# Rotary queries of a latent-attention layer: formed with channels on partitions, two heads at a time, with turned tables

## The chip, the core and the metric

One NeuronCore of a Trainium2 chip runs the whole kernel. The metric is the device time of one execution in microseconds; the shown time is the median of three runs. Everything is in 32-bit floats. A product that needs more precision than one pass of TensorE gives is made of three: each operand is split into a high half (rounded to the matmul's format, fp32r) and a low half (the rest), and high x low, low x high and high x high are added up in PSUM.

## The reference, cut to what matters

One layer: a token mixer of three branches and a gated MLP. The change lies in branch B, multi-head latent attention with 8 heads over 512 positions; each head has 128 plain channels and 64 rotary ones.

```python
def _apply_rope(x, cos, sin):
    x1, x2 = jnp.split(xf, 2, axis=-1)
    return jnp.concatenate([x1 * cos - x2 * sin, x2 * cos + x1 * sin], axis=-1)

def _mla(cq, ckv, kr, cos, sin, g_q, w_uq, g_kv, w_ukv):
    q = jnp.einsum('bsr,rhd->bshd', _rms_norm(cq, g_q), w_uq)
    kv = jnp.einsum('bsr,rhd->bshd', _rms_norm(ckv, g_kv), w_ukv)
    q_nope, q_rope = q[..., :QK_NOPE], q[..., QK_NOPE:]
    k_nope, v = kv[..., :QK_NOPE], kv[..., QK_NOPE:]
    q_rope = _apply_rope(q_rope, cos[:, :, None, :], sin[:, :, None, :])
    k_rope = _apply_rope(kr, cos, sin)
    scale = (QK_NOPE + QK_ROPE) ** -0.5
...
        s = (jnp.einsum('bqhd,bkhd->bhqk', q_nope[:, q0:q1], k_nope[:, :q1])
             + jnp.einsum('bqhd,bkd->bhqk', q_rope[:, q0:q1], k_rope[:, :q1]))
        s = s.astype(jnp.float32) * scale
...
        p = jax.nn.softmax(s, axis=-1).astype(v.dtype)
        outs.append(jnp.einsum('bhqk,bkhd->bqhd', p, v[:, :q1]))
```

## The kernel before, in words

All activations lie as tiles of 128 partitions x 512. The modulated input is hT (channels on partitions, 8 tiles, each with a high and a low half). The latent projections come out with positions on partitions, are normalised (cn), turned by TensorE transposes (ptc) and split into cT0, cT1 (the query latent, 256 channels) and cT2 (the key and value latent), each with h and l. The shared rotary key is turned in the same way: krT holds its high half twice, on partitions 0 to 63 and 64 to 127, krL its low half on 0 to 63 and zeros below.

Rotary queries of before: `rotary_queries` (L646) loads and splits the weight wqr as a whole, and for each of the four blocks of 128 positions forms pq (128 positions x 8 heads x 64 channels) by six matmuls of 512 columns, with the positions on partitions. VectorE multiplies pq by the scaled cosines and sines, cosQ and sinQ (made on ScalarE at L239 and L240), GpSimd subtracts and adds the halves into qro, and ScalarE and VectorE split the result into a high and a low half that lie side by side in a staging tile qst, 128 columns a head. `rotary_transposes` (L684) then turns one head: four transposes into ptq, one copy out into qrT (high half on partitions 0 to 63, low half on 64 to 127). Heads 0 to 3 are turned ahead of the head loop, heads 4 to 7 inside it, after the scores of the head four before.

`scores(h)` multiplies qrT by krL and by krT, so that high and low halves of the query meet the key in one pass each, and adds the plain part, q by k. In the head loop stand, for each head, the weights of the next head, its scores, the attention of the head before (`attend`), the projection of the next head (`project`: q and k from cT), one gate (24 matmuls, `mm_chunk`, L110) and the transposes of the softmax.

What sets the order: the code is written in program order, and a scheduler places each engine's instructions; an engine then takes its own in that order and waits at the first one whose inputs are not there. So an instruction that waits holds up all that stand behind it on its engine. PSUM has eight tiles (pool `pp`), taken in turn. Weights come by SyncE's DMA into three raw tiles; ScalarE casts the high half (L92), VectorE subtracts for the low half (L93), and two pairs of split tiles are used in turn.

Of the kernel before, what the change touches and what calls it, by code (L numbers as in the profile page):

```python
# [8 lines left out]
F32 = mybir.dt.float32  # L9
F32R = mybir.dt.float32r  # L10
# [40 lines left out]
def trunk(ctx: ExitStack, tc: tile.TileContext, A, out):  # L51
# [21 lines left out]
    def pt_t(name, dt=F32):  # L73
        return sb.tile([P, 512], dt, name=name, tag="pt", bufs=8)
# [4 lines left out]
    def f(ap):  # L79
        return ap.bitcast(F32)  # L80

    def load(src, n, name):
        raw = wp.tile([P, D], F32, name=name, tag="raw", bufs=3)
        with tc.issue_after(last_load[0]):
            nc.sync.dma_start(out=raw[:, :n], in_=src)
        return raw

    def wsplit(src, n, name):
        raw = load(src, n, name)
        hi = wp.tile([P, D], F32R, name=name + "h", tag="whi")  # L90
        lo = wp.tile([P, D], F32R, name=name + "l", tag="wlo")
        nc.scalar.copy(out=hi[:, :n], in_=raw[:, :n])  # L92
        ins = nc.vector.tensor_tensor(  # L93
            out=lo[:, :n], in0=raw[:, :n], in1=f(hi[:, :n]), op=ALU.subtract
        )
        last_lo[:] = [ins.ins]
        return hi, lo
# [7 lines left out]
    def mm3(o, wh, wl, xh, xl, start, stop):  # L105
        nc.tensor.matmul(o, wh, xl, start=start, stop=False)
        nc.tensor.matmul(o, wl, xh, start=False, stop=False)
        return nc.tensor.matmul(o, wh, xh, start=False, stop=stop)
# [80 lines left out]
    with tc.issue_after(x_load.ins):  # L189
# [13 lines left out]
    cosT, sinT, cosQ, sinQ = (  # L203
        const.tile([P, TT, 32], F32, name=name) for name in ("cosT", "sinT", "cosQ", "sinQ")
    )

    def angles():
        posf = const.tile([P, TT], F32, name="posf")
# [18 lines left out]
    def sines():  # L227
        nc.vector.tensor_scalar(
            out=ang, in0=ang, scalar1=3.1415925, scalar2=-3.1415925, op0=ALU.min, op1=ALU.max
        )  # L230
        nc.scalar.activation(sinT, ang, AF.Sin)
        nc.vector.scalar_tensor_tensor(
            out=kq, in0=ang, scalar=-1.0, in1=ang, op0=ALU.mult, op1=ALU.max
        )
        nc.vector.tensor_scalar(
            out=kq, in0=kq, scalar1=-1.0, scalar2=1.5707963267948966, op0=ALU.mult, op1=ALU.add
        )
        nc.scalar.activation(cosT, kq, AF.Sin)
        nc.scalar.activation(cosQ, cosT, AF.Copy, scale=SCALE)  # L239
        nc.scalar.activation(sinQ, sinT, AF.Copy, scale=SCALE)  # L240

    first_raw = {}
    first_acc = {}
# [327 lines left out]
    with after_split():  # L571
# [4 lines left out]
    ss = const.tile([P, TT, 2], F32, name="ss")  # L576
    rr = const.tile([P, TT, 2], F32, name="rr")
    cqn = []
    tA, tB, ro, krl = (
        act_t(name, F32)[:, : TT * 64].rearrange("p (t c) -> p t c", c=64)  # L580
        for name in ("tA", "tB", "ro", "krl")
    )
    kr = act_t("kr", F32).rearrange("p (t c) -> p t c", c=128)
# [52 lines left out]
    nc.scalar.copy(out=krF, in_=pt[:, 0:P])  # L636
    pt = ps("ptk")
    for t in range(TT):
        nc.tensor.transpose(pt[0:64, t * P : (t + 1) * P], krl[:, t, :], ident)
    nc.vector.tensor_copy(out=krL[0:64, :], in_=pt[0:64, :])  # L640
    nc.gpsimd.memset(f(krL[64:128, :]), 0.0)


    qrs = []

    def rotary_queries():  # L646
        wh, wl = wsplit(A["wqr"], D, "wqr")
        for t in range(TT):
            pq = ps("pq")
            ts_ = slice(t * P, (t + 1) * P)  # L650
            for k in range(2):
                c = slice(k * 512, (k + 1) * 512)
                mm3(pq, cT_hi[k][:, ts_], cT_lo[k][:, ts_], wh[:, c], wl[:, c], k == 0, k == 1)
            tA = pt_t("qtA")
            tB = pt_t("qtB")
            src = pq.rearrange("p (a b) -> p a b", b=32)
            for dst, tab in ((tA, cosQ), (tB, sinQ)):
                nc.vector.tensor_tensor(
                    out=dst.rearrange("p (a b) -> p a b", b=32), in0=src,
                    in1=tab[:, t : t + 1, :].broadcast_to([P, 16, 32]), op=ALU.mult,  # L660
                )
            vA = tA.rearrange("p (h a b) -> p h a b", a=2, b=32)
            vB = tB.rearrange("p (h a b) -> p h a b", a=2, b=32)
            ro = pt_t("qro")
            vo = ro.rearrange("p (h a b) -> p h a b", a=2, b=32)
            nc.gpsimd.tensor_tensor(
                out=vo[:, :, 0, :], in0=vA[:, :, 0, :], in1=vB[:, :, 1, :], op=ALU.subtract
            )
            nc.gpsimd.tensor_tensor(
                out=vo[:, :, 1, :], in0=vA[:, :, 1, :], in1=vB[:, :, 0, :], op=ALU.add  # L670
            )
            st = [act_t(f"qst{t}{i}", F32) for i in range(2)]
            for i in range(2):
                dst = st[i].rearrange("p (h a b) -> p h a b", a=2, b=64)
                s4 = ro[:, i * 256 : (i + 1) * 256].rearrange("p (h b) -> p h b", b=64)
                nc.scalar.copy(out=dst[:, :, 0, :].bitcast(F32R), in_=s4)
                nc.vector.tensor_tensor(
                    out=dst[:, :, 1, :], in0=s4, in1=dst[:, :, 0, :], op=ALU.subtract
                )
            qrs.append(st)  # L680

    qrT = []

    def rotary_transposes(h):  # L684
        pt = ps("ptq")
        for t in range(TT):
            nc.tensor.transpose(
                pt[:, t * P : (t + 1) * P], qrs[t][h // 4][:, (h % 4) * P : (h % 4 + 1) * P], ident
            )
        q = act_t(f"qrT{h}")  # L690
        if h % 2:
            nc.vector.tensor_copy(out=q, in_=pt)
        else:
            nc.scalar.copy(out=q, in_=pt)
        qrT.append(q)


    V = {}
# [878 lines left out]
```

## Time and profile before

| what | value |
| --- | --- |
| median of 3 runs | 963.16 us (961.87 to 963.17) |
| the profiled execution's own time | 962.52 us |
| its span, first to last instruction | 960.8 us |
| mean granted TensorE clock | 0.998 |
| HBM traffic | 116.83 MB read, 2.10 MB written, 124 GB/s over the span |

In the views, PE is TensorE's matmuls, PEld its weight loads, DVE VectorE, ACT ScalarE, POOL GpSimd, SP SyncE. A timeline row has the start and the duration in us, the engine, the source line, the operation, what is written and read, the form, and in brackets how long the engine had been idle and what ended that. Neighbouring matmuls overlap, so what one takes of PE's time is read from start to start. A row of a stretch has the stretch, its length, then for each engine the busy time and the count, PE's granted clock, the share of the DMA engines and GB/s.

The busy tenths of the span in 40 slices of 24 us; the rotary queries lie in the third and fourth slices, the head loop in the fourth to the ninth:

```profile
PE   7999999999999999999999999999999999999996
DVE  7967556456686566477333489576565564732368
ACT  4575656543333322233332245554444444322121
POOL 4752110122350023202212712021111121766653
```

### The profile page before, as it was taken

What the parts mean: (1) busy time and instruction counts of PE and PEld (TensorE: products, weight loads), DVE (VectorE), ACT (ScalarE), POOL (GpSimd) and SP (SyncE); (2) the same over time, 40 slices, a digit from 0 to 9 for tenths busy, and PEclk for the clock granted to TensorE, in tenths of its full rate; (3) what the DMA queues carried; (4) which work ended last, traced back from release to release, by engine and by line L of the source; (5) the groups of instructions that cost most, each with busy time, mean ns of one, the idle gap of its engine ahead of it and who ended that gap; (6) DMA issues with size and microseconds to landing.
All of it is one profiled execution on the core that took longest, in us unless ns stands there. A gap on an engine that the chain in (4) does not pass through costs nothing.

```text
span 960.8 us, 12195 instructions
## 1 busy us (share of the span) xinstructions
PE 947.2 (99%) x4583; PEld 800.2 (83%) x4583; DVE 585.0 (61%) x849; ACT 386.3 (40%) x637; POOL 284.6 (30%) x257
## 2 busy tenths in 40 slices
PE   7999999999999999999999999999999999999996
PEld 6988888888888888888888889988888888888885
DVE  7967556456686566477333489576565564732368
ACT  4575656543333322233332245554444444322121
POOL 4752110122350023202212712021111121766653
PEclk9999999999999999999999999999999999999999
DMA  9822112044435643564343550143434433342222
GB/s 330 309 63 89 50 61 82 24 124 162 146 106 197 202 128 88 164 199 151 111 130 111 148 181 23 47 129 116 126 110 130 133 113 107 106 132 92 89 87 88
DMA packets 46139, 119.72 MB, mean 125 GB/s; under 512 B 5504, under 2 KB 8960, under 8 KB 46080
## 3 DMA queue, kind: packets, MB, share of 16 engines
q1 hardware_dynamic: 45648, 118.39, 38.4%
q8 instruction: 36, 0.59, 0.2%
q10 hardware_dynamic: 432, 0.55, 0.2%
q14 instruction: 23, 0.19, 0.1%
HBM read 116.83 MB, written 2.10 MB: 124 GB/s over the span
## 4 chain that ended last, share of the span: by engine, by line
PE 93%; DVE 2%; POOL 1%; ACT 1%; DMA 1%; issue 1%; POOLq 0%; SPq 0%; ACTq 0%
PE pzu L114 7%; PE pzu L113 7%; PE pzu L116 7%; PE pg L113 4%; PE pg L114 4%; PE pg L116 4%; PE py L113 4%; PE py L114 4%; PE py L116 4%; PE pyd L1150 3%; PE pyd L1148 3%; PE pyd L1151 3%; PE lat L531 2%; PE pu L113 2%; PE pu L114 2%; PE pa L113 2%
## 5 line engine op out<-in xcount | busy, mean ns | idle before, releaser
L93 DVE TENSOR_TENSOR wupl<-wup,wuph 128x1024 fp32r<-128x1024 f32 x38 | 48.1, 1267 | 71.9 <-PE pzu L116 42.7
L1117 POOL TENSOR_TENSOR d<-d,gtfb 128x512 f32<-128x512 f32 x44 | 74.4, 1713 | 35.9 <-DMA d<-in_wdn 34.0
L1420 POOL TENSOR_TENSOR zc<-zc 128x512 f32<-128x512 f32 x22 | 29.6, 1348 | 174.6 <-ACT zc L1419 132.5
L1122 DVE TENSOR_TENSOR dl<-d,dh 128x1024 fp32r<-128x1024 f32 x18 | 28.6, 1588 | 56.2 <-PE pyd L1148 52.0
L92 ACT CAST wuph<-wup 128x1024 fp32r<-128x1024 f32 x38 | 39.9, 1051 | 47.1 <-PE pzu L114 47.1
L422 POOL TENSOR_TENSOR mg<-mg,th 128x512 f32<-128x512 f32 x16 | 31.4, 1959 | 85.8 <-DVE th L419 85.8
L92 ACT CAST wbh<-wb 128x1024 fp32r<-128x1024 f32 x24 | 25.3, 1054 | 74.0 <-PE py L114 55.3
L93 DVE TENSOR_TENSOR wgl<-wg,wgh 128x1024 fp32r<-128x1024 f32 x22 | 30.0, 1365 | 37.4 <-ACT wgh L92 18.4
L871 DVE SCALAR_TENSOR_TENSOR ada<-adar,cact,ada 128x512 f32<-128x512 f32 x56 | 49.0, 906 | 1.5 <-DMA adar<-in_ada 1.5
L786 POOL TENSOR_SCALAR pe<-pe,mx 128x128 f32<-128x128 f32 (+3 forms) x32 | 17.1, 537 | 96.0 <-DVE mx L785 59.9
L1121 ACT CAST dh<-d 128x1024 fp32r<-128x1024 f32 x18 | 19.0, 1053 | 61.6 <-PE pyd L1151 32.3
L1402 ACT ACTIVATE zc<-pzu,cols 128x512 f32<-128x512 f32 x44 | 34.2, 780 | 22.3 <-PE pzu L116 17.8
L93 DVE TENSOR_TENSOR wbl<-wb,wbh 128x1024 fp32r<-128x1024 f32 x24 | 30.9, 1288 | 14.6 <-ACT wbh L92 6.5
L1405 DVE SCALAR_TENSOR_TENSOR zc<-pzu,cols,zc 128x511 f32<-128x511 f32 x44 | 32.6, 742 | 4.0 <-ACT zc L1402 4.0
L1409 DVE SCALAR_TENSOR_TENSOR zc<-pzu,cols,zc 128x510 f32<-128x510 f32 x44 | 32.6, 744 | 0.8
L419 DVE SCALAR_TENSOR_TENSOR th<-th,py 128x512 f32<-128x512 f32 x16 | 11.0, 686 | 35.7 <-PE py L116 35.7
L92 ACT CAST wgh<-wg 128x1024 fp32r<-128x1024 f32 x22 | 23.2, 1054 | 23.1 <-PE pg L114 18.5
L1419 ACT ACTIVATE zc<-zc 128x512 f32<-128x512 f32 x22 | 13.9, 631 | 41.4 <-DVE zc L1409 41.3
L924 POOL TENSOR_TENSOR asum<-apad 128x527 f32<-128x527 f32 x8 | 12.7, 1587 | 54.2 <-ACT apad L919 27.6
L300 DVE SCALAR_TENSOR_TENSOR acc<-ada,cact,acc 128x256 f32<-128x256 f32 (+1 forms) x29 | 26.6, 917 | 1.1
L1096 POOL TENSOR_TENSOR oraw<-oraw,gttb 128x512 f32<-128x512 f32 x6 | 10.5, 1775 | 47.9 <-DMA oraw<-in_wo 43.8
L1117 POOL TENSOR_TENSOR o<-o,gttb 128x512 f32<-128x512 f32 x10 | 16.6, 1681 | 13.2 <-DMA o<-in_wo 10.4
(1547 smaller groups left out, 3109.8 us busy)
## 6 DMA issues: line engine op xcount, KB each, us to landing
wup<-in_wup SPq DMA_DIRECT2D x44, 512.0 KB, 3.6
adar<-in_ada SPq DMA_DIRECT2D x64, 256.0 KB, 4.0
wb<-in_wb SPq DMA_DIRECT2D x24, 512.0 KB, 3.6
wg<-in_wg SPq DMA_DIRECT2D x22, 512.0 KB, 3.6
d<-in_wdn SPq DMA_DIRECT2D x22, 512.0 KB, 3.6
ada<-in_ada1p SPq DMA_DIRECT2D x24, 256.0 KB, 4.7
wa<-in_wa SPq DMA_DIRECT2D x8, 512.0 KB, 3.5
wsg<-in_wsg SPq DMA_DIRECT2D x8, 512.0 KB, 3.7
```

Of the source, the lines that this page charges most:

```text
L92: nc.scalar.copy(out=hi[:, :n], in_=raw[:, :n])
L93: ins = nc.vector.tensor_tensor(out=lo[:, :n], in0=raw[:, :n], in1=f(hi[:, :n]), op=ALU.subtract)
L113: nc.tensor.matmul(o, wh[:, c], xl[k], start=k == 0, stop=False)
L114: nc.tensor.matmul(o, wh[:, c], xh[k], start=False, stop=False)
L116: nc.tensor.matmul(o, wl[:, c], xh[k], start=False, stop=k == KT - 1)
L422: nc.gpsimd.tensor_tensor(out=merged[m], in0=merged[m], in1=th, op=ALU.add)
L871: nc.vector.scalar_tensor_tensor(out=acc[n], in0=src, scalar=cact[:, k : k + 1], in1=acc[n], op0=ALU.mult, op1=ALU.add,)
L1117: nc.gpsimd.tensor_tensor(out=halves[n], in0=halves[n], in1=gt[n], op=ALU.mult)
L1402: nc.scalar.activation(t, pz, AF.Identity, bias=cols[:, cc + 3 : cc + 4], scale=cols[:, cc + 2 : cc + 3])
L1405: nc.vector.scalar_tensor_tensor(out=t[:, 1:512], in0=pz[:, 0:511], scalar=cols[:, cc + 1 : cc + 2], in1=t[:, 1:512], op0=ALU.mult, op1=AL ...
L1409: nc.vector.scalar_tensor_tensor(out=t[:, 2:512], in0=pz[:, 0:510], scalar=cols[:, cc : cc + 1], in1=t[:, 2:512], op0=ALU.mult, op1=ALU.add,)
L1420: nc.gpsimd.tensor_tensor(out=val, in0=val, in1=gate, op=ALU.mult)
```

## The change

The rotary queries are formed with the channels on partitions: `rotary(p)` makes pq as 128 channels of two heads (2p and 2p + 1) x 512 positions, with wqr as the left operand and cT as the right one, again by six matmuls of 512 columns. The rotation now runs over partitions: qtA is pq times a turned table cosR; qtB takes, for each group of 32 partitions, the neighbouring group of pq times a turned and signed table sinR (four products of 32 partitions); GpSimd adds them. ScalarE and VectorE split the result straight into qrT of both heads. In odd heads the low half now lies above the high one, and so krL holds the low half of the key twice in place of the zeros.

The tables are turned once, in `rotary_tables`: ScalarE writes each table with its sign and the scale into a wide tile (two writes of 256 elements a partition: cosRx, sinRx), TensorE turns it by four transposes into ptr, and ScalarE copies it out (cosR, sinR). The weight wqr is split in two halves, into tiles of its own (`rotary_weights`). The first pair of heads is formed ahead of the loop, the others after the scores of heads 0, 2 and 4. `rotary_queries`, `rotary_transposes`, cosQ, sinQ and the staging tiles are gone.

```diff
-        nc.scalar.activation(cosQ, cosT, AF.Copy, scale=SCALE)
-        nc.scalar.activation(sinQ, sinT, AF.Copy, scale=SCALE)
...
-    nc.gpsimd.tensor_tensor(out=krl, in0=ro, in1=kr[:, :, 0:64], op=ALU.subtract)
+    nc.gpsimd.tensor_tensor(out=krl[:, :, 0:64], in0=ro, in1=kr[:, :, 0:64], op=ALU.subtract)
+    nc.gpsimd.tensor_copy(out=krl[:, :, 64:128], in_=krl[:, :, 0:64])
...
-        nc.tensor.transpose(pt[0:64, t * P : (t + 1) * P], krl[:, t, :], ident)
-    nc.vector.tensor_copy(out=krL[0:64, :], in_=pt[0:64, :])
-    nc.gpsimd.memset(f(krL[64:128, :]), 0.0)
+        nc.tensor.transpose(pt[:, t * P : (t + 1) * P], krl[:, t, :], ident)
+    nc.vector.tensor_copy(out=krL, in_=pt)
...
+    def rotary_weights():
+        raw = load(A["wqr"], D, "wqr")
+        for k in range(2):
+            wh = act_t(f"wqr{k}h")
+            wl = act_t(f"wqr{k}l")
+            c = slice(k * 512, (k + 1) * 512)
+            nc.scalar.copy(out=wh, in_=raw[:, c])
+            nc.vector.tensor_tensor(out=wl, in0=raw[:, c], in1=f(wh), op=ALU.subtract)
+            wqr.append((wh, wl))
+
+    def rotary_tables():
+
+        for nm, src, signs in (("cosR", cosT, (1.0, 1.0)), ("sinR", sinT, (-1.0, 1.0))):
+            wide = act_t(nm + "x", F32)
+            for g, sign in enumerate(signs):
+                nc.scalar.activation(
+                    wide.rearrange("p (t a b f) -> p t a b f", a=2, b=2, f=32)[:, :, :, g, :],
+                    src.rearrange("p t (a f) -> p t a f", a=1).broadcast_to([P, TT, 2, 32]),
+                    AF.Copy, scale=sign * SCALE,
                 )
...
+            pt = ps("ptr")
+            for t in range(TT):
+                ts_ = slice(t * P, (t + 1) * P)
+                nc.tensor.transpose(pt[:, ts_], wide[:, ts_], ident)
+            table = act_t(nm, F32)
+            nc.scalar.copy(out=table, in_=pt)
+            turns.append(table)
...
+    def rotary(p):
+        pq = ps("pq")
+        c = slice(p * P, (p + 1) * P)
+        for k in range(2):
+            wh, wl = wqr[k]
+            mm3(pq, wh[:, c], wl[:, c], cT_hi[k], cT_lo[k], k == 0, k == 1)
+        tA = pt_t("qtA")
+        tB = pt_t("qtB")
+        nc.vector.tensor_tensor(out=tA, in0=pq, in1=turns[0], op=ALU.mult)
+        for j in range(4):
+            o = slice(32 * j, 32 * j + 32)
+            i = slice(32 * (j ^ 1), 32 * (j ^ 1) + 32)
+            nc.vector.tensor_tensor(out=tB[o, :], in0=pq[i, :], in1=turns[1][o, :], op=ALU.mult)
+        nc.gpsimd.tensor_tensor(out=tA, in0=tA, in1=tB, op=ALU.add)
+        for h in range(2):
+            q = act_t(f"qrT{2 * p + h}")
+            hi = slice(64 * h, 64 * h + 64)
+            lo = slice(64 - 64 * h, 128 - 64 * h)
+            nc.scalar.copy(out=q[hi, :], in_=tA[hi, :])
+            nc.vector.tensor_tensor(out=q[lo, :], in0=tA[hi, :], in1=f(q[hi, :]), op=ALU.subtract)
+            qrT.append(q)
...
     attention_weights(0)
-    rotary_queries()
+    rotary_weights()
+    rotary_tables()
+    rotary(0)
     th0.append(gate(0, 4))
     project(0)
     values(0, (0, 1))
-    rotary_transposes(0)
     th0.append(gate(0, 5))
-    rotary_transposes(1)
     values(0, (2, 3))
-    for h in (2, 3):
-        rotary_transposes(h)
...
-        if h + 4 < H:
-            rotary_transposes(h + 4)
+        if h in (0, 2, 4):
+            rotary(h // 2 + 1)
```

Where the instructions stand. First TensorE, behind the turning of the rotary key (ptk), in the kernel before; line numbers of the changed kernel differ by two to four from those of before:

```order
L631 MATMUL ptk<-ident,kr 128x128 x4
L634 MATMUL ptk<-ident,krf 128x128
L639 MATMUL ptk<-ident,krl 64x128 x4
L106 MATMUL pq<-wqrl,cT0h 128x512 x2
L107 MATMUL pq<-wqrh,cT0l 128x512
L108 MATMUL pq<-wqrh,cT0h 128x512
```

The same place on TensorE in the changed kernel (cosRx and sinRx are the wide tables, pg the next gate):

```order
L636 MATMUL ptk<-ident,krl 128x128 x4
L666 MATMUL ptr<-ident,cosRx 128x128 x4
L666 MATMUL ptr<-ident,sinRx 128x128 x4
L106 MATMUL pq<-cT0l,wqr0h 128x512
L107 MATMUL pq<-cT0h,wqr0l 128x512
L108 MATMUL pq<-cT0h,wqr0h 128x512
L106 MATMUL pq<-cT1l,wqr1h 128x512
L107 MATMUL pq<-cT1h,wqr1l 128x512
L108 MATMUL pq<-cT1h,wqr1h 128x512
L113 MATMUL pg<-hT0l,wgh 128x512
```

The transposes of both tables stand between the key and the rotary matmuls, of which six are left here in place of 24.

ScalarE at the same place, in the kernel before:

```order
L733 CAST wqk0h<-wqk_871 128x384
L123 ACTIVATE cT0h<-ptc,cols 128x512
L123 ACTIVATE cT1h<-ptc,cols 128x512
L636 COPY krF<-ptk 128x128
L123 ACTIVATE cT2h<-ptc,cols 128x512
L632 CAST krT<-ptk 128x512
L92 CAST wvh<-wv 128x512
```

And in the changed kernel:

```order
L731 CAST wqk0h<-wqk_867 128x384
L123 ACTIVATE cT0h<-ptc,cols 128x512
L649 CAST wqr0h<-wqr 128x512
L123 ACTIVATE cT1h<-ptc,cols 128x512
L633 COPY krF<-ptk 128x128
L649 CAST wqr1h<-wqr 128x512
L123 ACTIVATE cT2h<-ptc,cols 128x512
L658 ACTIVATE cosRx<-cosT 128x8x32 x2
L629 CAST krT<-ptk 128x512
L668 COPY cosR<-ptr 128x512
L658 ACTIVATE sinRx<-sinT 128x8x32 x2
L668 COPY sinR<-ptr 128x512
```

The two casts of wqr and the writes and copies of the tables stand among the casts of cT; the writes of sinRx stand behind the copy of cosR.

In the head loop, ScalarE after the last exponential of head 0, in the kernel before (k1h and q1h belong to head 1, wgh to a gate):

```order
L782 ACTIVATE pe,mx<-sc,mx 128x512
L747 ACTIVATE q1h<-pqn 128x512
L120 CAST k1h<-pkn 128x512
L92 CAST wgh<-wg 128x1024
L752 ACTIVATE qk1f<-pqn 128x128
```

In the changed kernel (qrT_1118 and qrT_1121 are the rotary queries of heads 2 and 3):

```order
L780 ACTIVATE pe,mx<-sc,mx 128x512
L691 CAST qrT_1118<-qtA 64x512
L691 CAST qrT_1121<-qtA 64x512
L745 ACTIVATE q1h<-pqn 128x512
L92 CAST wgh<-wg 128x1024
L120 CAST k1h<-pkn 128x512
```

VectorE at this place in the changed kernel:

```order
L778 TENSOR_REDUCE mx<-sc 128x1
L681 TENSOR_TENSOR qtA<-pq,cosR 128x512
L685 TENSOR_TENSOR qtB<-pq,sinR 32x512 x2
L783 RECIPROCAL mx<-mx 128x1
L685 TENSOR_TENSOR qtB<-pq,sinR 32x512 x2
L783 RECIPROCAL mx<-mx 128x1
L692 TENSOR_TENSOR qrT_1118<-qtA,qrT_1118 64x512
L692 TENSOR_TENSOR qrT_1121<-qtA,qrT_1121 64x512
L746 SCALAR_TENSOR_TENSOR q1l<-pqn,q1h 128x512
L93 TENSOR_TENSOR wgl<-wg,wgh 128x1024
L121 TENSOR_TENSOR k1l<-pkn,k1h 128x512
```

The rotary work of the next pair stands ahead of q1 and k1, and the gate weights have come ahead of k1 on both engines.

More of the change, by code (lines that the diff above doesn't have):

```diff
@@ L202, in trunk @@
     )
-    cosT, sinT, cosQ, sinQ = (
-        const.tile([P, TT, 32], F32, name=name) for name in ("cosT", "sinT", "cosQ", "sinQ")
-    )
+    cosT, sinT = (const.tile([P, TT, 32], F32, name=name) for name in ("cosT", "sinT"))
     def angles():
@@ L578, in trunk @@
     cqn = []
-    tA, tB, ro, krl = (
+    tA, tB, ro = (
         act_t(name, F32)[:, : TT * 64].rearrange("p (t c) -> p t c", c=64)
-        for name in ("tA", "tB", "ro", "krl")
+        for name in ("tA", "tB", "ro")
     )
-    kr = act_t("kr", F32).rearrange("p (t c) -> p t c", c=128)
+    kr, krl = (act_t(name, F32).rearrange("p (t c) -> p t c", c=128) for name in ("kr", "krl"))
     for t in range(TT):
@@ L638, in trunk @@
     for t in range(TT):
-        nc.tensor.transpose(pt[0:64, t * P : (t + 1) * P], krl[:, t, :], ident)
-    nc.vector.tensor_copy(out=krL[0:64, :], in_=pt[0:64, :])
-    nc.gpsimd.memset(f(krL[64:128, :]), 0.0)
[L644 to L660, printed above, removed]
-                )
[L662 to L680, printed above, removed]
@@ L682, in trunk @@
-    qrT = []
[L684 to L695, printed above, removed]
+        nc.tensor.transpose(pt[:, t * P : (t + 1) * P], krl[:, t, :], ident)
@@ new lines, in trunk @@
+    nc.vector.tensor_copy(out=krL, in_=pt)
+    wqr = []
+    turns = []
+    def rotary_weights():
[15 more added lines that the diff above has]
+                    AF.Copy, scale=sign * SCALE,
+                )
+            pt = ps("ptr")
[5 more added lines that the diff above has]
+            turns.append(table)
```

## The prediction

> **What bounds the kernel now.** I read the page first (busy shares, chain of work), then the list of waits for PE, then the timelines of PE and ScalarE around the rotary queries.
>
> ```profile
> span 960.8 us, 12195 instructions
> PE 947.2 (99%) x4583; PEld 800.2 (83%) x4583; DVE 585.0 (61%) x849; ACT 386.3 (40%) x637; POOL 284.6 (30%) x257
> ...
> PE 93%; DVE 2%; POOL 1%; ACT 1%; DMA 1%; issue 1%; POOLq 0%; SPq 0%; ACTq 0%
> ...
> PE lat L485 <- DMA x<-in_x: 5.4, 1, 5.4
> ...
> 68.60:76.40 7.80, 7.80 (x46) 6.64 (x45) 5.46 (x8) 3.39 (x7) 0.00 (x0) 1.00 0.40 131
> 80.16 1.81 PE pg L116 x8
> ```
>
> PE is busy for 99% of the span and makes 93% of the chain; its only long wait is the 5.4 us for x at the start. In 68.60 to 76.40, where the rotary queries are formed, it is busy for all of 7.80 us. So a microsecond of PE work or PE waiting added here ends up in the time, and work of the other engines counts only where PE comes to wait for it. A 512-wide matmul's slot is 1.81 / 8 = 0.227 us (the 0.39 in other rows overlaps its neighbours).
>
> **What PE loses.** Thirty-two transposes of the staged queries go, eight of the tables come; the 24 rotary matmuls stay 24 of the same width, spread out.
>
> ```profile
> 70.34 0.60 PE L639 MATMUL ptk<-ident,krl 128*64 128x128 f32 x4
> 70.70 0.72 PE L106 MATMUL pq<-wqrl,cT0h 128*128 128x512 f32 x2
> ...
> 76.37 0.39 PE L113 MATMUL pg<-hT0l,wgh 128*128 128x512 f32 x1
> ...
> 96.96 0.60 PE L687 MATMUL ptq<-ident,qst 128*128 128x128 f32 x4
> 97.31 0.48 PE L106 MATMUL pqn<-cT0l,wqk1h 128*128 128x512 f32 x1
> 97.63 0.39 PE L106 MATMUL pkn<-cT2l,wqk1h 128*128 128x512 f32 x1
> ...
> L687 PE MATMUL ptq<-ident,qst x32: 270/272/273, 85.2 to 138.0; 128*128 128x128 f32 x32
> ```
>
> Four transposes take 96.96 to 97.31, 0.35 us, and the matmul behind them 0.32 instead of 0.227: 0.44 a group, 0.11 each. Net 24 x 0.11 = **2.64 us saved**. It cannot be under 24 x 0.0875 = 2.1 (0.35 / 4). The 24 matmuls of before took 70.70 to 76.37, 5.67 us, against 24 x 0.227 = 5.45; 0.09 of the rest follows the transposes, and about 0.1 is waiting for cT0l, which goes too.
>
> **What PE gains: two waits at the tables.** PE's new order is krl's transposes, four of cosRx, four of sinRx, then the first six rotary matmuls. PE takes its work in order, and ScalarE has to make each table first, at the places in ScalarE's order that are shown with the change.
>
> ```profile
> 57.09 0.30 ACT L240 ACTIVATE sinQ<-sinT 128x128 f32<-128x128 f32 x1
> 57.30 0.30 ACT L239 ACTIVATE cosQ<-cosT 128x128 f32<-128x128 f32 x1
> ...
> 61.82 0.92 ACT L601 ACTIVATE cn<-lat,rr 128x256 f32<-128x256 f32 x2
> ...
> 63.76 1.16 ACT L92 CAST wqrh<-wqr 128x1024 fp32r<-128x1024 f32 x1
> ...
> 69.69 0.69 ACT L123 ACTIVATE cT0h<-ptc,cols 128x512 fp32r<-128x512 f32 x1
> 70.27 0.69 ACT L123 ACTIVATE cT1h<-ptc,cols 128x512 fp32r<-128x512 f32 x1
> 70.84 0.27 ACT L636 COPY krF<-ptk 128x128 f32<-128x128 f32 x1
> 70.99 0.72 ACT L123 ACTIVATE cT2h<-ptc,cols 128x512 fp32r<-128x512 f32 x1
> 71.57 0.61 ACT L632 CAST krT<-ptk 128x512 fp32r<-128x512 f32 x1
> ...
> 94.64 0.59 ACT L694 CAST qrT<-ptq 128x512 fp32r<-128x512 f32 x1
> 95.12 0.53 ACT L733 CAST wqk1h<-wqk 128x384 fp32r<-128x384 f32 x1
> ```
>
> Slots, start to start: cT 0.58, krF 0.15, a 512-wide cast 0.48. PE's work ahead of this place does not change, so cT0h still starts at 69.69. Behind it now stand wqr0h (70.27 to 70.75), cT1h (to 71.32), krF (71.47), wqr1h (71.95), cT2h (72.53), and only then the two writes of cosRx. Each is 256 wide, a form that the trace has only in other uses: it lies between the 128-wide sinQ, 0.21 a slot, and cn's, 0.92 for two. I take 0.3, near the first, since cn also reads a scale from a column. So cosRx is there at 73.13, with 0.1 for its end 73.25. PE was done with krl at 70.70: **it waits 2.5 us** (2.35 to 2.85). Its four transposes then end 0.60 later, at 73.85; in ScalarE's queue the copy of cosR waits for them and holds sinRx behind it. The copy (0.48) and sinRx (0.6, 0.1 for the end) bring 75.05; PE was free at 73.25 + 0.44: **a second wait of 1.4 us** (1.2 to 1.7). The casts of wqr, which lay far ahead of need at 63.76, are now inside this chain. The low halves that DVE makes of wqr and cT each follow their ScalarE cast by a slot or two and are there before PE wants them at 75.5.
>
> **Two waits in the head loop.** After heads 0 and 4 the new rotary work of DVE, GpSimd and ScalarE stands ahead of the next head's k low half, which PE needs for its scores.
>
> ```profile
> 72.44 0.68 DVE L640 CAST krL<-ptk 64x512 fp32r<-64x512 f32 x1
> ...
> 74.78 0.39 PE L108 MATMUL pq<-wqrh,cT1h 128*128 128x512 f32 x1
> ...
> 75.21 0.69 DVE L658 TENSOR_TENSOR qtA<-pq,cosQ 128x512 f32<-128x512 f32 x1 [2.09 <-PE pq L108]
> 75.81 0.68 DVE L658 TENSOR_TENSOR qtB<-pq,sinQ 128x512 f32<-128x512 f32 x1
> ...
> 98.22 0.69 DVE L780 TENSOR_REDUCE mx<-sc 128x1 f32<-128x512 f32 x1
> ...
> 54.20 1.30 POOL L521 TENSOR_TENSOR hT7l<-hfull,hT7h 128x512 fp32r<-128x512 f32 x1 [1.60 <-ACT hfull L520]
> ...
> 103.34 1.05 ACT L92 CAST wgh<-wg 128x1024 fp32r<-128x1024 f32 x1
> 104.30 0.27 ACT L752 ACTIVATE qk1f<-pqn 128x128 f32<-128x128 f32 x1
> ...
> 105.17 1.22 DVE L93 TENSOR_TENSOR wgl<-wg,wgh 128x1024 fp32r<-128x1024 f32 x1 [1.09 <-ACT qk1f L758]
> 106.31 0.55 DVE L734 TENSOR_TENSOR wqk2l<-wqk,wqk2h 128x384 fp32r<-128x384 f32 x1
> ```
>
> krL's 64 partitions cost what 128 do, so the four 32-partition products cost a full 0.60 slot each. Count from S, where PE is through with head 0's scores (96.96 before). DVE's last maximum starts at S + 1.26 and takes a slot: 1.86. qtA and four qtB, 5 x 0.60, and two reciprocals (0.1 together, an estimate): 4.96. GpSimd adds, 1.3: 6.26. ScalarE: two casts and q1h, 3 x 0.48: 7.7; then the gate weights' wgh, 0.96, which now stands ahead of k1h: 8.66. DVE: wgl after wgh, 1.14: 9.8; then k1l, 0.60, and 0.1 for its end: 10.5. PE: 39 matmuls x 0.227 + ten transposes x 0.11 + 0.2 (an estimate) for krF's small product = S + 10.15. That is 0.35 of waiting. The hops from engine to engine are not yet in it: PE's last product at 74.78 is over at 75.17 and DVE starts at 75.21, so 0.04 to 0.05 each, seven of them 0.35. Together **0.7**. Head 4's chain has the same links and no slack more: 0.7 again. I keep 0 to 1.3 for each. After head 2 no full-width weight split stands there: nothing.
>
> **At nothing:** SyncE's loads keep their number and size, two neighbours swap; krl's copy falls into GpSimd's idle time; cosQ and sinQ leave ScalarE where PE does not wait for it. The rotary queries themselves have over ten microseconds before the scores want them.
>
> **The sum:** -2.64 - 0.1 + 2.5 + 1.4 + 0.7 + 0.7 = +2.6. The profiled execution took 962.52 (its span and 1.7 around it), so 965.1; on the median of the three, 963.16, it is 965.7. I say **965.5**. Ends of the terms: +0.8 (no waits in the loop, the tables' at their least) to +5.0 (2.1 saved, every wait at its most): 963.3 to 968.2.
>
> **Rivals.** *PE's clock falls.* From 68.60 to 75.5 PE would run only transposes and wait.
>
> ```profile
> 5.40:8.40 3.00, 3.00 (x8) 2.63 (x9) 1.00 1.04 393
> 8.40:11.40 3.00, 3.00 (x17) 2.91 (x16) 1.00 1.05 400
> ...
> 953.06 0.28 PE L108 MATMUL pye<-d21h,f21h 128*128 128x256 f32 x1
> ...
> 953.00:957.00 4.00, 0.34 (x3) 1.00 0.34 131
> 957.00:960.80 3.80, 0.00 (x0) 0.54 0.38 138
> ```
>
> The first warm-up products went at 8 in 3.0 us, then 17: PE starts at half pace. After its last matmul, over at 953.34, PEclk is 1.00 up to 957 and 0.54 beyond. So some four empty microseconds lower it, and one empty wait here is 2.5. If it fell, 3 to 6 us of half pace would lose 1.5 to 3: 967.0 to 968.5. [...]
>
> *The loop's waits do not come* (DVE or GpSimd a microsecond earlier): 2.6 - 1.4 = +1.2, 963.7 to 964.3.
>
> *Faster: the tables are ready in time.* If ScalarE got cosRx and sinRx out before PE comes to them, nothing but the 2.7 saved would stay: 959.8, with the loop's waits 961.2. It decides the sign from the point where the four waits add up to less than 2.7. For it speaks that sinT and cosT exist before 57.3; against it the order, in which five of ScalarE's instructions stand between cT0h and cosRx, and a copy that waits for PE between the tables.
>
> **How the numbers follow.** Forecast 0.55, clock 0.22, no loop waits 0.17, faster 0.06. The range reaches into the two middle rivals: **963.0 to 968.8**. A measurement of this kernel can tell about 0.2% from no change, so slower means over 965.1 and faster under 961.2. The forecast lies 0.4 above that edge: I count two thirds of it as slower, all of the clock, little of the third: 0.62 slower, 0.05 faster, 0.33 the same.
>
> **What would show it.** PE idle before ptr's cosRx about 2.5 us and before sinRx 1.4, both put down to ScalarE; PE waiting before the first score product with k1l and k5l, put down to DVE; eight transposes in place of 32; PEclk 1.00 throughout if the clock holds. The prediction is wrong if cosRx's writes start before 72, if PE does not stand still at ptr, or if the end of the kernel does not move with PE.

## The result, and the profile after

The changed kernel takes 971.76 us (median of 4 runs, 971.66 to 971.86), the kernel before 963.16 (961.87 to 963.61): ratio 1.0094, 95% interval 1.0082 to 1.0106. The forecast was 965.5, with a range of 963.0 to 968.8. It is slower, as forecast, but by 8.6 us in place of 2.3. The profiled execution took 971.84, a span of 970.1 against 960.8.

The page of the changed kernel (span, busy time and instructions, shares of the chain), and below it the list of PE's waits (who waits, for what; us in total, times, longest):

```profile
span 970.1 us, 12147 instructions
PE 950.3 (98%) x4559; PEld 802.5 (83%) x4559; DVE 592.8 (61%) x858; ACT 387.8 (40%) x638; POOL 281.3 (29%) x253
...
PE 87%; DVE 5%; ACT 3%; POOL 2%; DMA 2%; issue 1%; SPq 0%; POOLq 0%; DVEq 0%; ACTq 0%
```

```profile
PE ptr L666 <- ACT cosRx L658: 2.5, 1, 2.5
PE sc L771 <- DVE k1l L121: 1.9, 1, 1.9
PE ptr L666 <- ACT sinRx L658: 1.3, 1, 1.3
PE sc L771 <- DVE k5l L121: 1.1, 1, 1.1
```

PE has 24 instructions fewer (4559 against 4583) and yet is busy for 3.1 us more: it did less work at a lower pace. Four waits that were not there add up to 6.8 us. The lower pace shows in the windows view of the changed kernel (stretch, its length, busy us and instructions of each engine; then the granted clock, the DMA share and GB/s). The stretches are cut where the clock changed, and one stretch of 3.41 us ahead of each fall; all these edges lie whole multiples of 3.41 us apart:

```profile
71.81:75.22 3.41, 0.78 (x6) 0.42 (x4) 3.41 (x6) 3.14 (x9) 0.00 (x0) 1.00 0.61 201
75.22:78.64 3.42, 2.30 (x8) 2.01 (x9) 0.05 (x1) 1.66 (x4) 0.00 (x0) 0.50 0.41 145
78.64:82.05 3.41, 3.41 (x10) 2.64 (x9) 1.90 (x3) 0.00 (x0) 0.00 (x0) 0.50 0.00 0
...
109.36:112.77 3.41, 1.52 (x13) 1.28 (x12) 3.20 (x6) 3.41 (x9) 0.00 (x0) 1.00 0.13 19
112.77:116.18 3.41, 3.41 (x11) 2.95 (x10) 1.07 (x5) 0.27 (x1) 0.00 (x0) 0.50 0.54 195
```

Behind the stretch with the first wait at the tables PE runs at half clock for two windows (the second wait falls mostly into the first of them), behind the wait for k1l for one. In PE's timeline a 512-wide matmul goes every 0.43 us there (78.53 to 78.96) and every 0.23 us at full clock (82.70 to 82.93), so 46% of the busy time is lost: (2.30 + 3.41) x 0.46 = 2.6 us and 3.41 x 0.46 = 1.6 us. One more microsecond lies at the start. The row of cT's transposes in the PE timeline of the kernel before (start, us, engine, line):

```profile
68.60 1.36 PE L619 MATMUL ptc<-ident,cn 128*128 128x128 f32 x11
```

Of the changed kernel:

```profile
69.59 1.36 PE L616 MATMUL ptc<-ident,cn 128*128 128x128 f32 x11
```

PE's work is the same up to here, but the trace's first record of a full clock stands at 8.41 us before, at 10.37 after and at 10.14 in e7; from 8.40 to 10.30 PE got through 12 instructions before and 6 after. About half of these 1.96 us is the 0.99 by which cT's transposes start later. That is the luck of one execution and not the change, since e7, a kernel below that differs from the kernel before only behind this place, starts them at 69.47, 0.87 later: the profiled execution of before is the luckiest of all, and in the experiments' profiles the first full clock came between 9.4 and 11.3 us.

**The sum of the profile:** -2.7 for the transposes, +6.8 for the waits, +4.2 for the clock, +1.0 for the start: +9.3, and the span grew by 9.3.

### The profile page after: what moved, and what is told of

Read it like the earlier page. It is cut to its first block, busy times and chain, and to the rows that moved or that the text cites. A ratio compares the mean times of both kernels' runs of the same rounds, so it can differ in the third digit from the quotient of the medians.

```text
span 970.1 us, 12147 instructions
## 1 busy us (share of the span) xinstructions
PE 950.3 (98%) x4559; PEld 802.5 (83%) x4559; DVE 592.8 (61%) x858; ACT 387.8 (40%) x638; POOL 281.3 (29%) x253
## 4 chain that ended last, share of the span: by engine, by line
PE 87%; DVE 5%; ACT 3%; POOL 2%; DMA 2%; issue 1%; SPq 0%; POOLq 0%; DVEq 0%; ACTq 0%
PE pzu L114 7%; PE pzu L113 7%; PE pzu L116 7%; PE py L113 4%; PE py L114 4%; PE py L116 4%; PE pg L113 4%; PE pg L114 4%; PE pg L116 4%; PE pyd L1146 3%; PE pyd L1147 3%; PE pyd L1144 3%; PE lat L527 2%; PE pu L113 2%; PE pu L114 1%; PE pu L989 1%
## 5 line engine op out<-in xcount | busy, mean ns | idle before, releaser
L780 ACT ACTIVATE pe<-sc,mx 128x128 f32<-128x128 f32 (+3 forms) x32 | 16.7, 526 | 11.9 <-DVE mx L778 11.4
```

## The experiments

The windows at half clock are those of the profiled execution, without the end of the kernel, where PE has no more work; pth is a wait near the end that the kernel before has, too. The times before in these runs were 963.13 (15 runs, for e1 to e4), 963.48 (15 runs, e5 to e7), 964.46 (one, e8) and 963.76 (7 runs, e9 and e10).

| | time us | ratio to before, 95% | PE's waits over 0.5 us behind that for x | windows at half clock |
|---|---|---|---|---|
| changed kernel | 971.76 | 1.0094 (1.0082 to 1.0106) | ptr 2.5, 1.3; k1l 1.9; k5l 1.1 | 2 at the tables, 1 at k1l |
| e1 tables early | 967.33 | 1.0038 (1.0024 to 1.0051) | k1l 3.1; k5l 1.1 | 1 at k1l |
| e2 waits filled | 972.57 | 1.0085 (1.0069 to 1.0100) | k0l 3.5; k1l 1.6; k5l 1.1 | 2 at k0l |
| e3 loop late | 969.84 | 1.0059 (1.0043 to 1.0074) | ptr 2.5, 1.3; pth 0.7; wqk2h 0.6; k2l 0.6 | 2 at the tables |
| e4 = e1 and e3 | 964.93 | 1.0017 (1.0008 to 1.0026) | k1l 1.8; pth 0.7; pg 0.6 | none |
| e5 tables early, halves late | 961.06 | 0.9979 (0.9971 to 0.9988) | pth 0.7 | none |
| e6 one product for four | 966.68 | 1.0047 (1.0032 to 1.0062) | ptr 2.5, 1.3 | 2 at the tables |
| e7 before, 64 more transposes | 970.31 | 1.0078 (1.0064 to 1.0091) | pth 0.8 | none |
| e8 four full products | 969.97, one run | | ptr 2.5, 1.3; k1l 1.6; k5l 1.0; pth 0.7 | 2 at the tables |
| e9 one quarter | 971.49, one run | | ptr 2.5, 1.3; k3l 1.8; k1l 1.3; k5l 0.7 | 2 at the tables |
| e10 halves late alone | 966.90 | 1.0037 (1.0022 to 1.0052) | ptr 2.5, 1.3; pth 0.8 | 2 at the tables |

**e1: the tables written early.** The four writes move from `rotary_tables` into `sines`; the transposes stay.

```diff
         nc.scalar.activation(cosT, kq, AF.Sin)
+        for nm, src, signs in (("cosR", cosT, (1.0, 1.0)), ("sinR", sinT, (-1.0, 1.0))):
+            wides[nm] = act_t(nm + "x", F32)
+            for g, sign in enumerate(signs):
+                nc.scalar.activation(
...
     def rotary_tables():
...
-            wide = act_t(nm + "x", F32)
...
+            wide = wides[nm]
```

> The changed kernel, with the two wide tables (cosRx, sinRx) written by ScalarE right behind the sines, some 40 us before their transposes. Theory (the tables are late in ScalarE's queue, TensorE stands still for them, and the clock falls for that standing still): TensorE's waits at ptr, 2.5 and 1.3 us, are gone, the two half-clock windows from 75.2 to 82.0 us with them (about 2.7 us), the waits for k1l and k5l stay; 971.8 - 3.8 - 2.7 = about 965.3 us, granted clock full until 110 us. Rival A (the clock fell for the run of 29 transposes, not for the waits): the waits go, the half-clock windows stay, about 968.0 us. Rival B (the waits move to the next readers: pq, tB or qrT): over 970 us.

967.33 us. The waits at ptr are gone, and the half clock there with them. Rival A expected that the half clock would stay, and the windows view of e1 has none:

```profile
71.73:75.14 3.41, 3.41 (x23) 2.99 (x22) 3.41 (x6) 3.41 (x8) 0.00 (x0) 1.00 0.62 211
75.14:78.55 3.41, 3.41 (x17) 2.83 (x16) 0.42 (x1) 1.38 (x2) 0.00 (x0) 1.00 0.44 154
...
102.45:105.86 3.41, 0.87 (x8) 0.63 (x6) 3.35 (x5) 3.36 (x7) 0.16 (x1) 1.00 0.00 0
105.86:109.27 3.41, 2.89 (x11) 2.90 (x12) 2.45 (x6) 1.62 (x6) 0.00 (x0) 0.50 0.62 170
```

It missed the expected 965.3 by two microseconds. PE's wait for k1l grew from 1.9 to 3.1: PE comes to it 6.6 us sooner, but k1l starts only 5.5 us sooner (105.64 against 111.09): the chain that leads to it, whose links the next section names, moved up by less, since VectorE now takes the last maximum (at 97.18) between the narrow products.

**e2: the waits filled with other products**, so that PE does not stand still while the tables are as late as before.

```diff
             pt = ps("ptr")
+            for _ in range({"cosR": 8, "sinR": 4}[nm]):
+                nc.tensor.matmul(pt, cT_hi[0][:, :P], cT_hi[0], start=True, stop=True)
             for t in range(TT):
```

> The changed kernel, with 8 matmuls of 128x512 ahead of the cosRx transposes and 4 ahead of those of sinRx; they write what the transposes overwrite, and their operand (cT0h) is there by 71.4 us, so 1.8 and 0.9 us of the waits of 2.5 and 1.3 us are filled and nothing ends later. Theory (TensorE's standing still costs the clock): the tables come as late as before, the two half-clock windows are gone, 971.8 - 2.7 = about 969.1 us. Rival A (the clock falls for the run of transposes, which is as long as before): no gain, 971.5 to 972. Rival B (the clock falls for another engine's work, or at random): no gain either, or another place of the half-clock windows.

972.57 us, a miss: no gain. The clock did what the theory said, full in the stretch where the change lost it (71.30 to 74.71: PE busy 3.41 us, clock 1.00). But the order was planned anew: all twelve fillers stood together, cosRx's transposes slid from 74.4 to 78.5 us, sinR's copy from 77.5 to 85.3, and the delay came back as a wait of 3.5 us for k0l, with two half-clock windows behind it. It shows that the half clock goes where the standing still goes. One of its four executions came near the theory's 969.1: 969.15 us at a mean granted clock of 0.998, where the other three have 972.35 to 972.87 at 0.994 to 0.995. In the traces the end of the kernel, where PE is out of work, takes 0.0011 to 0.0026 off the mean, and each half-clock window another 0.0018, so this execution had no room for one in its middle. It has no trace, and the 3.2 us and more by which it is shorter also hold the luck of its start.

**e3: the rotary work of the loop written behind project(h+1).**

```diff
-        if h in (0, 2, 4):
-            rotary(h // 2 + 1)
         if h + 1 < H:
             project(h + 1)
+        if h in (0, 2, 4):
+            rotary(h // 2 + 1)
```

> The changed kernel, with rotary(p) of the head loop written behind project(h+1) instead of ahead of it, so that VectorE and ScalarE split k1 and k5 before they turn the queries. Theory (k1l and k5l wait behind the rotary's own instructions in VectorE's queue): waits of 1.9 and 1.1 us at sc go, and with the first of them the half-clock window from 112.8 to 116.2 us (about 1.7 us): 971.8 - 3.0 - 1.7 = about 967.1 us; a wait of up to 0.8 us at k2l may take its place (967.9). Rival A (the half-clock window has another cause): 968.8 us and the window stays. Rival B (the split of the gate's weights on VectorE, not the rotary, keeps k1l back): waits at k1l and k5l of over 1 us stay, over 970 us.

969.84 us against 967.1. The waits for k1l and k5l and the half clock from 112.8 us are gone, but waits of 0.4 to 0.6 us stand at three other places (wqk2h, k2l, wqk6h), and pth has 0.7. The place of the cost was right; the edit moved part of it on.

**e4: e1 and e3 together.**

> Tables written behind the sines and rotary(p) behind project(h+1), both edits together. Theory: no wait of TensorE over 0.5 us after the input, no half-clock window, so the whole saving of 24 transposes is left: 963.2 - 2.7 = about 960.5 us, less than the kernel before; at most 0.8 us more for a wait at k2l. Rival (what was lost lies elsewhere too, for instance in the later entry of about 1 us seen in the profiled execution): 961.5 to 963 us.

964.93 us against 960.5. In the profile the clock is full throughout, but 1.8 us of waiting for k1l are back: a miss of the theory and of its rival. The scheduler put the narrow products ahead of k1l in VectorE's queue, though the code has them behind project(h+1); in e3, with the same order of the code, they stand behind k1l. VectorE's timeline of e4:

```profile
100.91 0.69 DVE L750 SCALAR_TENSOR_TENSOR q1l<-pqn,q1h 128x512 fp32r<-128x512 f32 x1 [3.34 <-ACT q1h L749]
101.52 0.68 DVE L685 TENSOR_TENSOR qtA<-pq,cosR 128x512 f32<-128x512 f32 x1
102.22 2.79 DVE L689 TENSOR_TENSOR qtB<-pq,sinR 32x512 f32<-32x512 f32 x4
105.04 0.69 DVE L121 TENSOR_TENSOR k1l<-pkn,k1h 128x512 fp32r<-128x512 f32 x1
```

Two of its eleven executions have a mean granted clock of 0.996 where the other nine have 0.998, more than the end of the kernel accounts for and as much as one half-clock window takes; they took 966.11 and 966.30 us, on the mean 1.5 us more than the nine. They have no trace, but this fits a fall behind the wait for k1l in some executions only, at about the cost that the pace gives (1.6).

VectorE stands idle for 3.34 us ahead of q1l: that is where the products belong, early, and only what follows GpSimd's add belongs behind k1. That is e5.

**e5: tables early; in the loop the products stay early and only the casts and low halves of qrT go behind project(h+1).** Beside e1's edit:

```diff
         nc.gpsimd.tensor_tensor(out=tA, in0=tA, in1=tB, op=ALU.add)
+        return p, tA
+
+    def halves(p, tA):
         for h in range(2):
...
         if h in (0, 2, 4):
-            rotary(h // 2 + 1)
+            turned = rotary(h // 2 + 1)
         if h + 1 < H:
             project(h + 1)
+        if h in (0, 2, 4):
+            halves(*turned)
```

> Tables written behind the sines; in the head loop the rotary products and the add stay ahead of project(h+1), but the two casts and the two low halves of qrT (lines 689 to 692) come behind it. Theory (q1h and k1h stand in ScalarE's queue behind the casts of qrT, which wait for GpSimd's add; DVE's four narrow products are the head of that chain): no wait of TensorE over 0.6 us after the input, granted clock full, so the saving of 24 transposes shows: 963.1 - 2.7 = about 960.5 us, 961.3 with a wait of 0.3 to 0.6 us at po. Rival A (VectorE's products alone keep k1l back): a wait of 1 to 2 us at k1l stays, 962 to 963.5 us. Rival B (moved waits: PTl or o0l late): 962 to 964 us.

961.06 us, ratio 0.9979 (0.9971 to 0.9988): 2.4 us faster than before, as expected. This is the saving of the 24 transposes with 0.3 us of waiting off it (its list of PE's waits, whole, behind that for x):

```profile
PE pth L1271 <- ACT xr L1258: 1.0, 2, 0.7
PE po L106 <- DVE PTl L121: 0.3, 1, 0.3
```

The wait for xr at the end stands in the kernel before too, at 0.3 us in its profile and 0.8 in e7's, which changes nothing there. ScalarE's timeline of e5 shows what moved:

```profile
100.06 0.60 ACT L752 ACTIVATE q1h<-pqn 128x512 fp32r<-128x512 f32 x1 [0.87 <-PE pqn L108]
100.78 1.06 ACT L92 CAST wgh<-wg 128x1024 fp32r<-128x1024 f32 x1
101.75 0.57 ACT L120 CAST k1h<-pkn 128x512 fp32r<-128x512 f32 x1
...
102.39 1.25 ACT L698 CAST qrT<-qtA 64x512 fp32r<-64x512 f32 x2
```

q1h and k1h wait only for their products; in the changed kernel they stood behind qrT (rows in the next section).

**e10: the halves late, the tables as late as the change has them**, the fourth corner.

> The changed kernel, with the casts and low halves of qrT behind project(h+1) in the head loop, and the tables as late as the change has them. Theory: the two waits at the tables (2.5 and 1.3) and their half clock (2.7) stay, k1l and k5l cost nothing: 961.1 + 3.8 + 2.7 = about 967.6 us. Rival (the gain of doing both was more than the sum of its parts): over 969 us.

966.90 us, near the theory's number. Of the 10.7 us between the changed kernel and e5, the halves alone give 4.9 and the early tables alone 4.4; together they give 1.4 more than the sum (the runs were made on different chips, whose times before differ by up to 0.6). With the tables early alone, the wait for k1l grew by 1.2.

One thing moved that no edit asked for. In the changed kernel, e1, e2, e8 and e9, which all wait for k1l, VectorE splits the next gate's weights (wgl) ahead of k1l; in e3, e5, e6 and e10, which do not, it splits them behind k1l, as in the kernel before. So no run moves the halves alone with the gate's split left where it was. An estimate from the changed kernel's timelines: with only the halves of qrT behind, q1h could start at 104.1, when its product is there, and k1l would be done by 108.0, ahead of PE at 109.9; with only wgh and wgl behind, k1l would be done at 110.3, some 0.4 of the 1.9 left. In e4 wgl stands behind k1l, and PE waits 1.8 us all the same.

**e6: one product of 128 partitions in place of four of 32**; the exchange of the halves is left out.

```diff
-        for j in range(4):
...
-            nc.vector.tensor_tensor(out=tB[o, :], in0=pq[i, :], in1=turns[1][o, :], op=ALU.mult)
+        nc.vector.tensor_tensor(out=tB, in0=pq, in1=turns[1], op=ALU.mult)
```

> The changed kernel, with one product of 128 partitions for qtB in place of four of 32; it leaves out the exchange of the halves. Theory (in the head loop the four narrow products are what makes the chain to k1l and k5l too long): VectorE's stretch for qtB falls from 2.8 to 0.7 us, the waits at k1l (1.9) and k5l (1.1) go, the half-clock window from 112.8 us too, the waits and the half clock at the tables stay: 971.8 - 3.0 - 1.7 = about 967 us. Rival (the chain's other links, GpSimd's add, ScalarE's casts and the gate weights' split, set it): the waits shrink by under 1 us each, over 969 us.

966.68 us, the theory's number. With 2.1 us less on VectorE (and wgl behind k1l) the waits for k1l and k5l and the half clock behind k1l are gone; those at the tables are unchanged.

**e7: do transposes count for the clock?** The kernel before, with 64 more of them and no wait.

```diff
     for t in range(TT):
-        nc.tensor.transpose(pt[0:64, t * P : (t + 1) * P], krl[:, t, :], ident)
+        for _ in range(17):
+            nc.tensor.transpose(pt[0:64, t * P : (t + 1) * P], krl[:, t, :], ident)
```

> The kernel before, with each of the four transposes of krl done 17 times in place of once: 64 more transposes in a row, nothing that waits. Theory (the clock falls for the time in which TensorE stands still; transposes count as busy): granted clock as before, 64 x 0.11 = 7.0 us more, about 970.1 us. Rival (transposes do not count as busy, so that a run of 9 us of them is as good as idle): TensorE at half clock for one to three windows of 3.4 us from about 73 us on, 972 to 975 us.

970.31 us, 6.8 more than before: 64 x 0.107. The PE timeline of e7 has them in one row, the windows view has the clock of that stretch:

```profile
71.22 7.59 PE L640 MATMUL ptk<-ident,krl 128*64 128x128 f32 x68
```

```profile
71.58:74.99 3.41, 3.41 (x34) 3.41 (x32) 1.82 (x3) 1.48 (x4) 0.00 (x0) 1.00 0.71 211
74.99:78.40 3.41, 3.41 (x33) 3.41 (x32) 0.00 (x0) 0.00 (x0) 0.00 (x0) 1.00 0.00 0
```

The first of these windows holds hardly anything but transposes, the second nothing else, and the clock stays full; the rotary matmuls behind them are at full pace, too. So these transposes, of 128x64 in fp32 and listed in the trace as matmuls with an identity, count as work: PE is busy for 3.41 of 3.41 us and the clock is 1.00. In these runs it was the standing still that cost the clock.

**e8 and e9: why does a narrow product take 0.70 us?** In e8 each product covers all 128 partitions; the exchange is left out.

```diff
-            nc.vector.tensor_tensor(out=tB[o, :], in0=pq[i, :], in1=turns[1][o, :], op=ALU.mult)
+            nc.vector.tensor_tensor(out=tB, in0=pq, in1=turns[1], op=ALU.mult)
```

> The changed kernel, with each of the four narrow products of qtB done on all 128 partitions; the exchange of the halves is left out. It asks what makes a narrow product cost more than a full one. If it is that they follow each other into the same tile: four products take 2.8 us again (0.70 each, no overlap), and the waits at k1l and k5l stay at 1.9 and 1.1 us. If it is the part of the partitions: 0.60 each, 2.5 us for four, and each of the two waits 0.3 to 0.4 us shorter.

2.86 us for four, no overlap, but this settles nothing: each overwrites what the one ahead of it wrote, which the narrow ones of the change do not, and may be held for that alone. (The wait for k1l is 0.3 us shorter all the same, as was expected for the other cause; 0.1 of that is qtA, which takes 0.59 here.) Hence e9, in which four products of 32 partitions start at partition 0 and write four tiles; the rest of the turn is left out.

```diff
-        for j in range(4):
...
+        for dst in (act_t("qtC", F32), act_t("qtD", F32), act_t("qtE", F32), tB):
+            nc.vector.tensor_tensor(out=dst[0:32, :], in0=pq[0:32, :], in1=turns[1][0:32, :], op=ALU.mult)
```

> The changed kernel, with four products of 32 partitions that all start at partition 0, in pq, sinR and the output, each into a tile of its own; the add takes 32 partitions, and the rest of the rotary turn is left out. It asks why a narrow product takes 0.70 us and doesn't overlap the next. If it is the change of the starting partition from one product to the next: 0.60 each here, 2.5 us for four. If it is the part of the partitions as such: 0.70 each, 2.8 us. The time itself says nothing here, since the tiles that are added delay others.

VectorE's timeline of e9:

```profile
80.72 0.67 DVE L683 TENSOR_TENSOR qtC<-pq,sinR 32x512 f32<-32x512 f32 x1
81.31 0.67 DVE L683 TENSOR_TENSOR qtD<-pq,sinR 32x512 f32<-32x512 f32 x1
```

0.59 and 0.60 from start to start (the third starts at 81.91): as narrow as in the change, and they overlap. So it is not the few partitions. Nor is it that the narrow products of the change share the tile qtB: qtA and the first of them write different tiles in both kernels, and are 0.61 apart in e9 (80.11 to 80.72), 0.71 in the changed kernel (80.12 to 80.83). What differs there is the partition at which pq is read (32 in the changed kernel, 0 in e9), so in these runs the 0.10 us go with the change of the starting partition: the products that start at a new partition each time take 2.79 us for four, 0.70 each without overlap, and those that all start at 0 are 0.67 long and 0.59 to 0.60 apart.

## Why the prediction was wrong in size, point by point

- **The saving, 2.64:** right. e5, in which nearly all else is taken out, is 2.4 us faster than before with 0.3 us of waiting left.
- **The tables, 2.5 and 1.4:** right, 2.46 and 1.29. ScalarE's timeline of the changed kernel, with cosRx's writes at 73.60 (the step was counted to 72.53, with the start some 1 us earlier than in this execution) and the copy that holds sinRx behind it:

```profile
73.60 0.74 ACT L658 ACTIVATE cosRx<-cosT 128x256 f32<-128x256 f32 x2
74.21 0.60 ACT L629 CAST krT<-ptk 128x512 fp32r<-128x512 f32 x1
75.08 0.58 ACT L668 COPY cosR<-ptr 128x512 f32<-128x512 f32 x1 [0.27 <-PE ptr L666]
75.56 0.72 ACT L658 ACTIVATE sinRx<-sinT 128x256 f32<-128x256 f32 x2
```

- **The loop, 0.7 and 0.7:** the right place and chain, measured 1.9 and 1.1. The chain to k1l in the changed kernel, VectorE's, ScalarE's and GpSimd's timelines:

```profile
100.93 0.16 DVE L783 RECIPROCAL mx<-mx 128x1 f32<-128x1 f32 x1 [0.29 <-ACT pe L780]
...
101.25 0.69 DVE L778 TENSOR_REDUCE mx<-sc 128x1 f32<-128x512 f32 x1
101.86 0.68 DVE L681 TENSOR_TENSOR qtA<-pq,cosR 128x512 f32<-128x512 f32 x1
102.55 1.38 DVE L685 TENSOR_TENSOR qtB<-pq,sinR 32x512 f32<-32x512 f32 x2
...
104.16 1.40 DVE L685 TENSOR_TENSOR qtB<-pq,sinR 32x512 f32<-32x512 f32 x2
...
109.94 1.23 DVE L93 TENSOR_TENSOR wgl<-wg,wgh 128x1024 fp32r<-128x1024 f32 x1 [0.21 <-ACT wgh L92]
111.09 0.68 DVE L121 TENSOR_TENSOR k1l<-pkn,k1h 128x512 fp32r<-128x512 f32 x1
```

```profile
106.96 1.26 ACT L691 CAST qrT<-qtA 64x512 fp32r<-64x512 f32 x2 [4.20 <-POOL qtA L686]
108.25 0.60 ACT L745 ACTIVATE q1h<-pqn 128x512 fp32r<-128x512 f32 x1
108.87 1.05 ACT L92 CAST wgh<-wg 128x1024 fp32r<-128x1024 f32 x1
109.82 0.58 ACT L120 CAST k1h<-pkn 128x512 fp32r<-128x512 f32 x1
```

```profile
105.64 1.28 POOL L686 TENSOR_TENSOR qtA<-qtA,qtB 128x512 f32<-128x512 f32 x1 [0.84 <-DVE qtB L685]
```

  PE was through with head 0's scores at S = 99.60. The forecast had the last maximum start at S + 1.26; it started at S + 1.65: a reciprocal ahead of it waits for ScalarE's exponentials, and these began at S + 0.39 (99.99), where they had begun at S before (96.96). The four narrow products were put at 0.60 each, "krL's 64 partitions cost what 128 do": a price that holds for one narrow instruction (krL's is 0.68 us long) and for a row that starts at partition 0 (e9, 0.59 to 0.60 apart), not for a row of them that start at different partitions. They took 0.70, and so did qtA ahead of them, 0.5 in all. The two casts and q1h, put at 3 x 0.48, took 1.91 (106.96 to 108.87), another 0.5. With hops between, k1l started at S + 11.5 in place of S + 9.8, or 10.15 with the 0.35 that the forecast had for hops. So the mechanism stood, and the term was mis-sized in its row of slots, taken from instructions in another neighbourhood: 1.9 and 1.1 in place of 0.7 and 0.7, 1.6 us together.

- **The clock:** this is the step that failed, and where the range was missed: the sum has nothing for it, and the runs show 2.6 + 1.6 us. It was named as a rival with 0.22, and 967.0 to 968.5; its 3 to 6 us of half pace were the author's estimate, and the changed kernel has 5.7 us of PE work at half pace at the tables and 3.4 at k1l. It was held unlikely because the gate was read off the tail of before, "some four empty microseconds lower it, and one empty wait here is 2.5". No run was needed to see how that could fail: an entirely empty stretch shows that emptiness is enough, not that it is needed. Half clock followed a window with 0.78 us of work in it, and one with 1.52 (below). That the clock could fall a second time, in the loop, was not thought of, since a wait of 0.7 us was expected there; one of 1.9 us did it. Both clock terms make most of the difference between +2.6 and +8.6; the loop's waits make 1.6 of it.
- **Why the clock could have fallen at all:** the rival put the whole stretch down to transposes and waits alike. e7 takes the transposes out of it: 7.6 us of nothing else leave the clock full.
- **The reference run:** the sum stood on an execution whose first full clock came at 8.4 us, and was brought to the median by 0.6. That was right in kind; the changed kernel's profiled execution had 1.0 us less luck.

## What to carry to other kernels

On PE, busy for 98% of the span here, a wait cost its length and, if it was long enough, the pace of what followed. Behind waits of 1.9 us (changed kernel) and 3.1 (e1) one window of 3.41 us went at half clock, behind 2.5 with 1.3 and behind 3.5 (e2) two; behind 1.8 (e4, e9) and 1.6 (e8) none in the profiles. So, by these runs, price a wait of some 2 us or more as one or two windows at half clock more: no gap ahead of these falls was a whole window. When work is moved into a loop, look for what it puts in front of the next step in each engine's queue: here a cast that waits 4.20 us for an add of 1.28 stood ahead of two that had their inputs, and to move the casts and the low halves behind was worth 4.9 us, together with the gate's split, which moved along. A table that depends on nothing late is written where its inputs are made, not where it is used.

## What the runs showed of the hardware

**The clock fell without an idle window.** PE's busy time in single windows of 3.41 us at full clock, and what the next window had: half clock behind 0.66 us (e3), 0.78, 0.87 (e1), 0.98 (e2) and 1.52 (changed kernel, wait of 1.9); full clock behind 1.54 (e3, near its end), 1.59 (e4, wait of 1.8), 1.61 (e1, near its end) and 1.76 (e8, wait of 1.6). So among these nine windows half clock goes with 1.52 us of work and less, full clock with 1.54 and more. Whether the share of work or the longest gap in a window decides, they do not show: in each of these windows nearly all the idle time is one gap, and a gap of 1.89 us (changed kernel) was followed by half clock, one of 1.87 (e3) by full. The windows of e4 and of e3:

```profile
103.04:106.45 3.41, 1.59 (x15) 1.43 (x14) 3.35 (x5) 1.23 (x3) 1.27 (x1) 1.00 0.00 0
106.45:109.87 3.42, 3.42 (x21) 3.08 (x20) 3.34 (x8) 2.61 (x5) 0.00 (x0) 1.00 0.37 83
```

```profile
959.84:963.26 3.42, 1.54 (x13) 1.34 (x12) 3.28 (x10) 0.00 (x0) 1.52 (x1) 1.00 0.40 153
963.26:966.67 3.41, 0.00 (x0) 0.00 (x0) 2.36 (x4) 0.51 (x1) 1.95 (x2) 1.00 0.18 68
```

The way back took more work: at half clock, windows with 2.30 (changed kernel), 2.35 (e2) and 2.55 us (e3) of work were followed by another at half, and one with 2.89 (e1) by full clock. So one long wait cost two windows where a second wait followed it, as at the tables (2.5 and 1.3 us), or where it lasted into the next window, as in e2 (3.5). Ahead of the falls in the middle of these kernels no window was idle: the longest empty stretch within one was 2.54 us (e1). The windows do not start with the kernel: the first full clock came at another time in each profile, 8.41 us before and 10.37 after. So a wait can lie in one window, as the 1.9 us of the changed kernel (109.94 to 111.83, in 109.36 to 112.77), or be cut in two by an edge, as the second one at its tables (75.05 to 76.34, edge at 75.22); and by an estimate from e4's granted clocks (0.996 in two of eleven executions, 0.998 in nine) one of 1.8 us fell on either side of the line.

**The start differs from one profiled execution to the next.** The first full clock came between 8.4 and 11.3 us in the profiled executions of these kernels, and about half of the difference is in the time (0.99 of 1.96 us in the changed kernel, 0.87 of 1.73 in e7, both against before): up to about 1.5 us, an estimate. The kernel before spreads over 961.9 to 964.7 in the runs of e1 to e4; how much of that is the start no run shows, since only one execution of each kernel has a trace.
